# ln(dt) in the bias of the scan's exponential, and plain rows copied by ScalarE

## The chip, the cores and the metric

The kernel runs on one core of one Trainium2 chip. The metric is the device time of one execution in microseconds (us). A core has five engines, each with an instruction queue of its own that is worked off in order: TensorE (PE in the profile; its weight loads are shown apart as PEld), VectorE (DVE), ScalarE (ACT), GpSimd (POOL) and SyncE (SP, which here only issues transfers). They meet at semaphores. SBUF is the working memory, PSUM the memory into which TensorE writes its results.

## The reference

One step of a hybrid encoder layer is computed for 1024 prompt tokens and 64 sample tokens: an input projection, then a state-space scan and a differential attention beside each other, their gated mix, and a feed-forward block with a convolution. The change lies in the scan. Its core in the reference, for one chunk of tokens (`xc` the rows, `dtc` the step sizes, `bc` and `cc` the two state projections):

```python
acum = jnp.cumsum(dtc * a_neg, axis=1)
seg = acum[:, :, None] - acum[:, None, :]
decay = jnp.exp(jnp.where(causal[None, :, :, None, None], seg, -jnp.inf))
xdt = xc * dtc[..., None]
cb = jnp.einsum('blgn,bsgn->blsg', cc, bc)
y = jnp.einsum('blsg,blsge,bsgep->blgep', cb, decay, xdt)
y = y + jnp.einsum('blgn,bgepn->blgep', cc, state) * jnp.exp(acum)[..., None]
to_end = jnp.exp(acum[:, -1:] - acum)
state = state * jnp.exp(acum[:, -1])[..., None, None] + jnp.einsum('blgn,blge,blgep->bgepn', bc, to_end, xdt)
```

The step sizes `dt` are a softplus, so they are positive. There are 32 heads in 4 groups of 8; a head has 64 columns and a state of 64 x 128.

## The kernel before, in words

All data are 32-bit floats. Large products are made of three TensorE products each (high part by high part, high by low, low by high); the scan's own products are plain 32-bit ones.

The program runs through stages. First the input projection, q, k, z and some gates first, in an order of steps written out by hand (`INPUT`): each step sends PE's products and takes out their results on ACT and DVE. Woven into it, by a queue of small jobs (`beside`, `take_turn`), runs `steps` (lines 705 to 754), which makes everything that the scan needs of the step sizes: the softplus into `dt_tok`, the cumulated exponents by a product with a triangle, their negative `nacum` (line 732), the decay of the whole chunk `decs` (line 737), and `dtw`, which is `dt` times the decay to the chunk's end (lines 738 to 740). `dt_tok` and `dtw` are the two halves of one tile `dtt`. The cumulated exponents are also turned and stored to DRAM (`a_sc`, lines 742 to 753). `one_by_one` issues the parts of `steps` one at a time behind a recent copy or read of the projection's results.

Then comes attention, with further tiles of the projection and the convolution woven in (`fill`), and then the scan (lines 1265 to 1447), with gate tiles and two branch products woven in by the same `fill`. The scan goes over 4 groups, and in each over 9 chunks (8 of 128 tokens, one of 64): 36 steps. Each has a front, which runs one step ahead, and a back.

`front` (lines 1287 to 1311): ACT takes the exponential of the row of exponents `bc` that came from `a_sc` (`e2`, line 1294). PE turns the rows of four tiles into one PSUM tile `tr` (line 1297), turns one state projection and multiplies the two into the PSUM tile `cb` (lines 1299 and 1300), which ACT copies (line 1302). DVE multiplies `tr` by `dt` and by `dtw` in one instruction over both halves of `dtt`, which gives `xdt` and `xw`, two halves of the tile `xx` (lines 1303 to 1306; two buffers of it). POOL masks `bc` above the diagonal with -1e30 (line 1307). ACT takes eight exponentials of it, one for each head, with `nacum` as bias (line 1309), and DVE multiplies them by `cb` (line 1310).

`back` (lines 1313 to 1340): PE multiplies `xdt` by the eight decays into `yi` (line 1318) and the old state into `ye` (line 1324); DVE adds the two (lines 1325 and 1326), or ACT copies `yi` where there is no state (line 1328). PE makes the state's addition from `xw` (line 1330); POOL and DVE, or ACT at a group's start, make the new state (lines 1333 to 1337). After three chunks at most `gated`, `normed` and `scaled` finish a span of tokens and store it to `y_sc` (lines 1342 to 1374).

The tiles `tr`, `cb` and `yi` have one PSUM bank each; the woven-in products have three. They share the DVE and ACT queues with the scan: their results are taken out by line 232 (ACT) or 234 (DVE).

The order of the instructions on each engine is drawn up when the kernel is built: the order of the program text gives priorities, `high_priority` raises some, and a simulation with modelled durations decides what each engine issues next. On the chip that order is fixed.

Of the kernel before, what the change touches and what calls it, by code (L numbers as in the profile page):

```python
# [11 lines left out]
AF = mybir.ActivationFunctionType  # L12
ALU = mybir.AluOpType
# [76 lines left out]
def hybrid_layer(ctx: ExitStack, tc: tile.TileContext, xT, xt, prm, cst, rope, wvd, win, wbs, wba, wout, wup, wdn,  # L90
                 ckT, cv, st0, yT, kT, v, ssm, conv, ffn):
    nc = tc.nc
    V, S, G, PE = nc.vector, nc.scalar, nc.gpsimd, nc.tensor
    act = S.activation
# [166 lines left out]
    nacum, decs = (dq.tile([P, 9, 32], F32, name=n) for n in ("nacum", "decs"))  # L261
    dtt = dq.tile([P, 2, 9, 32], F32, name="dtt")
    dt_tok, dtw = dtt[:, 0], dtt[:, 1]
# [12 lines left out]
    def stat(w):  # L276
        t = ps1.tile([P, 512], F32, name="st", tag="st")
        return t[:, :w]
# [197 lines left out]
    def row(tag, name, dt=F32):  # L476
        if tag in ("fa", "fs", "fu"):
            w = {"fa": KT * P, "fs": 4 * P, "fu": HT}[tag]
            return rows_l.tile([P, w], dt, name=name, tag=tag, bufs=IN_ROWS[tag])
        w = {"ss": T}.get(tag, HT)  # L480
        return rows_r.tile([P, w], dt, name=name, tag=tag, bufs=IN_ROWS[tag])
# [223 lines left out]
    def steps():  # L705
        flat = [four[:, 288 * i : 288 * (i + 1)] for i in range(3)] + [row("fx", "dt2")[:, :288]]
        da, e, t, t2 = (x.rearrange("p (a b) -> p a b", b=32) for x in flat)
        u = dtw
        act(e, u, AF.Abs)
        act(e, e, AF.Exp, scale=-1.0)  # L710
        V.tensor_scalar_add(t, e, 2.0)
        V.reciprocal(t, t)
        V.tensor_tensor(out=t, in0=t, in1=e, op=ALU.mult)
        V.tensor_tensor(out=t2, in0=t, in1=t, op=ALU.mult)
        yield
        V.tensor_scalar(e, t2, 1.0 / 17, None, ALU.mult)
        for n in (15, 13, 11, 9, 7, 5, 3):
            V.scalar_tensor_tensor(e, e, 1.0 / n, t2, ALU.add, ALU.mult)
        yield
        V.scalar_tensor_tensor(e, e, 1.0, t, ALU.add, ALU.mult)  # L720
        V.tensor_scalar_max(u, u, 0.0)
        V.scalar_tensor_tensor(dt_tok, e, 2.0, u, ALU.mult, ALU.add)
        an = four[:, 864:896]
        act(an, par[:, O_AL : O_AL + 32], AF.Exp)
        V.scalar_tensor_tensor(da, dt_tok, -1.0, an.unsqueeze(1).to_broadcast([P, 9, 32]), ALU.mult, ALU.mult)
        V.memset(da[TS:, 8, :], 0.0)
        yield
        flat = lambda x: x.rearrange("p a b -> p (a b)")
        pa = stat(288)
        with tc.issue_after(seen["mm"].ins):  # L730
            PE.matmul(pa, tri, flat(da), start=True, stop=True)
        V.tensor_scalar(flat(nacum), pa, -1.0, None, ALU.mult)
        yield
        pl = stat(288)
        with tc.issue_after(seen["mm"].ins):
            PE.matmul(pl, ones, flat(da), start=True, stop=True)
        act(flat(decs), pl, AF.Exp)
        V.tensor_tensor(out=flat(dtw), in0=pl, in1=flat(nacum), op=ALU.add)
        act(dtw, dtw, AF.Exp)
        V.tensor_tensor(out=dtw, in0=dtw, in1=dt_tok, op=ALU.mult)  # L740
        yield
        for c, w in WIDE:
            af = row("fc", "af")[:32, :w]
            pf = stat(512)
            with tc.issue_after(seen["mm"].ins):
                for i in range(c // P, -(-(c + w) // P)):
                    n = min(P, T - i * P)
                    PE.matmul(pf[:32, i * P - c : i * P - c + n], da[:n, i], tri[:n, :n], start=True, stop=True)
            V.tensor_copy(af, pf[:32, :w])
            m = (min(c + w, TP) - c) // P  # L750
            load(out=a_sc[c // P : c // P + m].rearrange("c h t -> h c t"), in_=af[:, : P * m].rearrange("h (c t) -> h c t", t=P))
            if c + w > TP:
                load(out=a_sc[8, :, :TS], in_=af[:, P * m : P * m + TS])
            yield
# [165 lines left out]
    for at, (p, s) in enumerate(rest):  # L920
# [8 lines left out]
        if s == 1 and p in LATER:  # L929
            split_part(LATER[p], seen["copy"], seen["read"])  # L930
    beside = chain(cached_keys(), one_by_one(steps()))
    for n in range(1, len(INPUT)):
        blocks = blocks_of(n + 1) if n + 1 < len(INPUT) else None
# [331 lines left out]
    with (tc.tile_pool(name="sin", bufs=1) as sin, tc.tile_pool(name="sp", bufs=1) as sp,  # L1265
# [21 lines left out]
        def front(g, ch, o, bx, xs, bc):  # L1287
            L = P if ch < 8 else TS
            cs = slice(o, o + L)
            h8 = slice(8 * g, 8 * g + 8)  # L1290
            e2 = sp.tile([P, 4, P], F32, name="e2", tag="e2", bufs=3)
            for u in range(2):
                half = slice(64 * u, 64 * u + 64)
                act(e2[half, :, :L], bc.rearrange("p (j u) t -> p u j t", u=2)[half, u, :, :L], AF.Exp)
            tr = psi.tile([P, 512], F32, name="tr", tag="tr")
            for j in range(4):
                PE.transpose(tr[:L, P * j : P * (j + 1)], xs[:, j, cs], ident)
            cb = psi.tile([P, 512], F32, name="cb", tag="cb")
            PE.transpose(cb[:L, 0:P], bx[:, 0, cs], ident)
            PE.matmul(cb[:L, P : P + L], bx[:, 0, cs], bx[:, 1, cs], start=True, stop=True)  # L1300
            b_cb = sp.tile([P, 2 * P], F32, name="b_cb", tag="b_cb", bufs=3)
            S.copy(b_cb[:L, : P + L], cb[:L, : P + L])
            xx = sp.tile([P, 2, 8, 64], F32, name="xx", tag="xx", bufs=2)
            xdt, xw = xx[:, 0], xx[:, 1]
            tr3 = tr[:L].rearrange("p (e q) -> p e q", e=8).unsqueeze(1).to_broadcast([L, 2, 8, 64])
            V.tensor_tensor(out=xx[:L], in0=tr3, in1=dtt[:L, :, ch, h8].unsqueeze(3).to_broadcast([L, 2, 8, 64]), op=ALU.mult)
            G.affine_select(bc[:L, :, :L], bc[:L, :, :L], [[0, 8], [1, L]], ALU.is_ge, -1e30, base=0, channel_multiplier=-1)
            for e in range(8):
                act(bc[:L, e, :L], bc[:L, e, :L], AF.Exp, bias=nacum[:L, ch, 8 * g + e : 8 * g + e + 1])
            V.tensor_tensor(out=bc[:L, :, :L], in0=bc[:L, :, :L], in1=b_cb[:L, P : P + L].unsqueeze(1).to_broadcast([L, 8, L]), op=ALU.mult)  # L1310
            return L, cs, bc, e2, b_cb, xdt, xw
# [66 lines left out]
        def scan():  # L1378
# [9 lines left out]
            def begin(n):  # L1388
                if n == len(steps):
                    return None  # L1390
                if n and n + 2 < len(steps):
                    asked.append(ask(*steps[n + 2]))
                i, g, c, w, o = steps[n]
                return front(g, (c + o) // P, o, *got[i], asked[n])
# [592 lines left out]
```

## Time and profile before

| | |
|---|---|
| median of 3 runs | 2413.97 us (2413.55 to 2416.66) |
| profiled execution | 2411.51 us, span 2409.7 us |
| instructions | 48636 |
| preparation of the exponents (`steps`) | about 188 to 228 us after the start |
| scan, first to last product of `yi` | 1138.7 to 1467.0 us |

The span goes from the first to the last instruction. The profile's rows give, for a group of instructions, the source line, engine, operation, what is written and read, the count, the busy time and the mean duration of one in ns, and then how long the engine had stood idle just before them and which work ended that idle time. A row of the timeline gives the start and the duration in us. A `q` behind an engine's name is its queue: it waits or issues a transfer, and the engine itself is idle.

### The profile page before, as it was taken

The page shows a single profiled execution, that of the slowest core. Times are in us where ns is not written, and L with a number is a line of the kernel's source. Part 1 is how long each engine was busy: PE and PEld are TensorE (multiplying, and loading weights), DVE is VectorE, ACT ScalarE, POOL GpSimd, SP SyncE. Part 2 cuts the span into 40 slices and gives each one's busy share as a digit, 9 for nine tenths or more (in the row PEclk, how much of TensorE's full clock was granted, in tenths as well). Part 3 has the DMA queues.
Part 4 walks back from the last instruction along what each step waited for, and adds up shares of the span by engine and source line. Part 5 has one row for each costly group of instructions (what it writes and reads, how often), then busy time and mean ns, then how long its engine had stood idle before and what let it go on. Part 6 is the DMA issues. An engine that isn't in the chain of part 4 may idle for free. (4 is left out here: it accounts for less than half of the span.)

```text
span 2409.7 us, 48636 instructions
## 1 busy us (share of the span) xinstructions
PE 2373.4 (98%) x18649; PEld 2302.2 (96%) x18649; DVE 1729.4 (72%) x2938; ACT 1201.2 (50%) x2600; POOL 634.4 (26%) x689
## 2 busy tenths in 40 slices
PE   8999999999999999999999999999999999999998
PEld 8999999999999999999898889999899999999998
DVE  4678887646858768884898886647866667677765
ACT  6444454335656656665566664334443343353442
POOL 0032443320100000001223220012254455443444
PEclk9999999999999999999999999999999999999999
DMA  7873768526554444435978956663124324357876
GB/s 246 273 245 129 266 221 303 170 102 208 160 156 161 151 144 137 148 110 188 353 266 280 331 192 205 203 215 130 65 82 164 138 98 162 127 191 211 246 184 106
DMA packets 288170, 449.74 MB, mean 187 GB/s; under 512 B 35833, under 2 KB 178306, under 8 KB 287938
## 3 DMA queue, kind: packets, MB, share of 16 engines
q1 hardware_dynamic: 258594, 387.00, 48.6%
q0 software_dynamic: 11040, 26.34, 5.4%
q10 hardware_dynamic: 18304, 33.30, 3.7%
q8 instruction: 147, 2.41, 0.4%
q14 instruction: 85, 0.70, 0.1%
HBM read 294.03 MB, written 152.50 MB: 185 GB/s over the span
## 5 line engine op out<-in xcount | busy, mean ns | idle before, releaser
L170 PE MATMUL mm<-b,w_hi 128*128 128x272 f32 x1376 | 407.7, 296 | 0.0
L171 PE MATMUL mm<-b,w_hi 128*128 128x272 f32 x1376 | 405.8, 295 | 0.0
L172 PE MATMUL mm<-b,w_lo 128*128 128x272 f32 x1376 | 403.8, 294 | 0.0
L171 PEld LDWEIGHTS mm<-b,w_hi 128*128 128x128 f32 x1376 | 259.5, 189 | 5.9 <-issue 4.1
L170 PEld LDWEIGHTS mm<-b,w_hi 128*128 128x128 f32 x1376 | 259.3, 188 | 5.3 <-issue 2.7
L172 PEld LDWEIGHTS mm<-b,w_lo 128*128 128x128 f32 x1376 | 259.0, 188 | 5.2 <-issue 4.2
L1629 PE MATMUL mx<-m,w_hi 128*128 128x272 f32 x792 | 152.3, 289 | 2.5 <-DVE hb L1667 1.3
L420 DVE TENSOR_TENSOR wh<-w_f,wh 128x512 fp32r<-128x512 f32 (+1 forms) x156 | 149.7, 960 | 0.7 <-ACT wh L419 0.7
L1629 PE MATMUL mx<-n,wh 128*128 128x272 f32 x1056 | 141.7, 288 | 1.3 <-DVE u L1656 0.9
L1629 PEld LDWEIGHTS mx<-n,wh 128*128 128x128 f32 x1056 | 135.7, 188 | 1.7 <-DVE u L1656 1.2
L1132 ACT ACTIVATE p_t<-sc,mx 128x512 f32<-128x512 f32 (+6 forms) x144 | 106.0, 739 | 59.0 <-DVE mx L1123 33.0
L1629 PEld LDWEIGHTS mx<-m,w_hi 128*128 128x128 f32 x792 | 124.4, 188 | 2.9 <-DVE hb L1667 1.5
L170 PE MATMUL mx<-b,w_hi 128*128 128x272 f32 x416 | 123.4, 297 | 1.1 <-ACT w_hi L155 0.8
L172 PE MATMUL mx<-b,w_lo 128*128 128x272 f32 x416 | 121.6, 294 | 0.0
L563 POOL TENSOR_TENSOR ws<-w_f 128x512 f32<-128x512 f32 (+1 forms) x51 | 69.0, 1354 | 195.4 <-DMA w_f<-in_wdn_dram 84.2
L171 PE MATMUL mx<-b,w_hi 128*128 128x272 f32 x416 | 120.4, 290 | 0.0
L1009 DVE SCALAR_TENSOR_TENSOR cc<-pre,par,cc 128x544 f32<-128x544 f32 (+1 forms) x144 | 111.2, 772 | 8.2 <-ACT cc L1007 6.9
L156 DVE TENSOR_TENSOR w_lo<-w_f,w_hi 128x1024 fp32r<-128x1024 f32 (+1 forms) x74 | 92.5, 1251 | 33.9 <-ACT w_hi L155 33.7
L1629 PE MATMUL mx<-m,w_lo 128*128 128x272 f32 x396 | 114.2, 289 | 0.0
L1638 ACT ACTIVATE cc<-pre,par 128x544 f32<-128x544 f32 (+1 forms) x44 | 37.2, 846 | 150.0 <-DVE pre L1673 149.1
L419 ACT CAST wh<-w_f 128x512 fp32r<-128x512 f32 (+1 forms) x156 | 95.3, 613 | 26.1 <-POOL w_f L569 6.8
L155 ACT CAST w_hi<-w_f 128x1024 fp32r<-128x1024 f32 (+1 forms) x74 | 77.6, 1049 | 56.1 <-PE mm L171 30.3
(466 smaller groups left out, 7124.8 us busy)
## 6 DMA issues: line engine op xcount, KB each, us to landing
w_f<-in_win_dram SPq DMA_DIRECT2D x40, 512.0 KB, 3.9
w_f<-in_wup_dram SPq DMA_DIRECT2D x80, 256.0 KB, 2.6
w_f<-in_win_dram SPq DMA_DIRECT2D x76, 256.0 KB, 3.2
bc<-a_sc SPq DMA_DIRECT2D x32, 512.0 KB, 7.0
b<-y_sc SPq DMA_DIRECT2D x24, 544.0 KB, 8.2
h_sc<-hb SPq DMA_DIRECT2D x44, 272.0 KB, 2.1
ht<-h_sc SPq DMA_DIRECT2D x22, 544.0 KB, 4.6
t_sc<-ht SPq DMA_DIRECT2D x22, 544.0 KB, 3.0
```

What stands on the lines that cost most here:

```text
L155: S.copy(hi, w)
L156: V.tensor_tensor(out=lo, in0=w, in1=hi, op=ALU.subtract)
L170: PE.matmul(ps, a_hi, b_hi, start=i == 0, stop=False)
L171: PE.matmul(ps, a_hi, b_lo, start=False, stop=False)
L172: PE.matmul(ps, a_lo, b_hi, start=False, stop=i == n - 1)
L419: S.copy(hi, src)
L420: V.tensor_tensor(out=lo, in0=src, in1=hi, op=ALU.subtract)
L563: G.tensor_tensor(out=s1, in0=q21, in1=q22, op=ALU.add)
L1009: V.scalar_tensor_tensor(cc[:, :m], pre[:, i : i + m], cw(i), cc[:, :m], ALU.mult, ALU.add)
L1132: act(p_t[:n, :nk], sc[c][:n, :nk], AF.Exp, bias=mx[:n, c : c + 1], accum_out=dst)
L1629: PE.matmul(ps, w[x][:, c], b[y][:, k], start=start and k == i == 0, stop=k == 3 and i == 2, skip_group_check=not start)
L1638: act(cc[:, :n], pre[h][:, :n], AF.Identity, bias=col(O_FB + f), scale=cw(0))
```

## The change

In `steps`, after `dtw` is made, `dt_tok` is raised to at least 1e-37, replaced by its logarithm on ACT, and added to `nacum`. In `front` the exponentials of line 1309 therefore give the decay times `dt`, and `xdt` holds the plain rows: ACT copies them from `tr`. DVE multiplies `tr` only by `dtw`, for `xw`. The shapes of PE's products, the loads and the stores stay as they are.

```diff
         V.tensor_tensor(out=dtw, in0=dtw, in1=dt_tok, op=ALU.mult)
+        V.tensor_scalar_max(dt_tok, dt_tok, 1e-37)
+        act(dt_tok, dt_tok, AF.Ln)
+        V.tensor_tensor(out=nacum, in0=nacum, in1=dt_tok, op=ALU.add)
         yield
...
             xdt, xw = xx[:, 0], xx[:, 1]
-            tr3 = tr[:L].rearrange("p (e q) -> p e q", e=8).unsqueeze(1).to_broadcast([L, 2, 8, 64])
-            V.tensor_tensor(out=xx[:L], in0=tr3, in1=dtt[:L, :, ch, h8].unsqueeze(3).to_broadcast([L, 2, 8, 64]), op=ALU.mult)
+            tr3 = tr[:L].rearrange("p (e q) -> p e q", e=8)
+            S.copy(xdt[:L], tr3)
+            V.tensor_tensor(out=xw[:L], in0=tr3, in1=dtw[:L, ch, h8].unsqueeze(2).to_broadcast([L, 8, 64]), op=ALU.mult)
```

## The prediction

> **What bounds the kernel now.** I read the page's totals first, then the chain that ended last, the stretches around the two places of the change, and the list of who waited for whom.
>
> ```profile
> span 2409.7 us, 48636 instructions
> PE 2373.4 (98%) x18649; PEld 2302.2 (96%) x18649; DVE 1729.4 (72%) x2938; ACT 1201.2 (50%) x2600; POOL 634.4 (26%) x689
> PE 7%; issue 1%; POOL 0%; DVE 0%; POOLq 0%; ACT 0%; DVEq 0%
> ```
>
> PE is busy for 2373.4 of 2409.7 us; 36.3 us is all that it ever stands idle. The chain's shares add up to some 8% of the span: it covers the last 200 us (0.08 x 2409.7), where the scan is long over. So the scan moves the end only by the time that PE loses inside it. The stretches (columns: length, busy time of PE, weight loads, DVE, ACT, POOL, clock, DMA share, GB/s) show how much that is:
>
> ```profile
> 185.00:235.00 50.00, 49.37 (x377) 47.27 (x376) 40.29 (x72) 21.72 (x43) 12.79 (x9) 1.00 0.37 129
> 235.00:640.00 405.00, 402.18 (x3153) 397.59 (x3152) 288.38 (x502) 191.07 (x391) 114.29 (x119) 1.00 0.63 208
> 1121.00:1475.00 354.00, 350.73 (x2849) 314.88 (x2848) 290.37 (x380) 219.27 (x528) 90.78 (x68) 1.00 0.82 277
> ...
> 1201.00:1241.00 40.00, 40.00 (x340) 36.10 (x339) 36.11 (x50) 28.60 (x67) 13.82 (x10) 1.00 0.77 267
> 1241.00:1281.00 40.00, 40.00 (x328) 36.32 (x328) 37.68 (x53) 23.18 (x56) 11.58 (x7) 1.00 0.81 262
> 1281.00:1321.00 40.00, 40.00 (x317) 35.98 (x316) 38.08 (x56) 27.21 (x61) 12.12 (x7) 1.00 0.82 272
> 1321.00:1361.00 40.00, 38.11 (x317) 33.69 (x316) 32.70 (x44) 22.91 (x55) 9.75 (x8) 1.00 1.08 375
> ```
>
> The first row is where the decay's exponents are prepared, the third is the whole scan (36 steps, so 354 / 36 = 9.8 us a step). In the scan PE is idle for 354 - 350.73 = 3.3 us, over half of it in the last row (1.9 us). DVE is the busiest of the others, 290.4 us or 82%, and 90 to 95% between 1201 and 1321; yet PE there shows 40.00 of 40, because the projections that are woven in give it work. ACT has 219.3 us, 62%. The clock is 1.00 throughout. PE's waits in the scan, by who ended them:
>
> ```profile
> PE yi L1318 <- ACT y L1328: 1.9, 1, 1.9
> PE tr L1297 <- DMA in<-x_sc: 0.7, 1, 0.7
> PE yi L1318 <- DVE y L1326: 0.6, 1, 0.6
> ```
>
> These three make 3.2 of the 3.3 us. A lighter DVE can win at most 3.3 us here, 0.14% of 2414. Differences below 0.2% (4.8 us) are about what a measurement of this kernel can't tell from no change.
>
> **The change part by part.** *The preparation.* It adds a maximum and a sum on DVE and a logarithm on ACT, all over 128x288. Their nearest rows:
>
> ```profile
> L711 DVE TENSOR_SCALAR st<-st x1: 301/301/301, 190.6 to 190.6; 128x288 f32<-128x288 f32 x1
> L740 DVE TENSOR_TENSOR dtt<-dtt x1: 674/674/674, 216.8 to 216.8; 128x288 f32<-128x288 f32 x1
> L739 ACT ACTIVATE dtt<-dtt x1: 447/447/447, 216.3 to 216.3; 128x288 f32<-128x288 f32 x1
> 0.74 1.28 ACT L285 ACT_TABLE_LOAD   x1 [0.74 <-PEq L1975]
> 217.87 1.28 ACT L822 ACT_TABLE_LOAD   x1
> ```
>
> DVE gets 0.30 + 0.67 = 0.97 us, ACT 0.45 us. Both table loads name the set of logarithm and exponential, and none lies between them, so the logarithm at about 217.5 finds its table. The stretch 185 to 235 has PE at 49.37 of 50 with DVE at 40.3, ACT at 21.7: both additions lie under it. Behind the new sum on DVE, which waits for the logarithm, stand the copies of line 749, whose PSUM tile the next small product needs. If that cover is gone the cost is the whole detour, 0.97 + 0.45 = 1.4 us, once. The new exponents are first read 900 us later. I take 0; ends 0 and 1.4.
>
> *The rows.* Per step one DVE product of 1024 columns goes; a copy of 512 columns on ACT and a DVE product of 512 columns come. All three read `tr` in PSUM.
>
> ```profile
> L1306 DVE TENSOR_TENSOR xx<-tr,dtt x36: 1206/1216/1226, 1128.8 to 1454.1; 128x1024 f32<-128x1024 f32 x32, 64x1024 f32<-64x1024 f32 x4
> L1325 DVE TENSOR_TENSOR y<-ye,e 128x512 f32<-128x512 f32 x28 | 19.1, 683 | 7.3 <-DMA y_sc<-y 5.2 <-PE ye L1324 2.0
> L1328 ACT COPY y<-yi x4: 578/586/588, 1143.1 to 1394.1; 128x512 f32<-128x512 f32 x4
> L1294 ACT ACTIVATE e<-bc 64x512 f32<-64x512 f32 x64 | 40.2, 629 | 14.1 <-DMA bc<-a_sc 7.4 <-DVE y L1325 5.2 <-DMA o_sc<-ol 1.0
> ```
>
> The remaining product has the form of line 1325, one operand in PSUM and one in SBUF: 0.683 us. DVE saves 36 x (1.216 - 0.683) = 19.2 us and falls to 271.2 us (77%). If the broadcast factor made it as slow as line 1306, the saving would be 0. The copy has the form of line 1328: ACT gets 36 x 0.586 = 21.1 us and rises to 240.4 us (68%). Work on both stays far below 354 us. PE's products, loads and DMAs stay as they are: no queue gets or loses a transfer.
>
> *What the saved DVE time buys.* I looked at the two waits where DVE or ACT held PE up.
>
> ```profile
> 1309.63 1.21 DVE L1306 TENSOR_TENSOR xx<-tr,dtt 128x1024 f32<-128x1024 f32 x1
> 1310.76 0.94 DVE L1371 TENSOR_TENSOR y<-y,zin 128x768 fp32r<-128x768 f32 x1
> ...
> 1310.72 2.31 SPq L214 DMA_DIRECT2D b<-y_sc  x2
> 1313.12 2.75 SPq L1374 DMA_DIRECT2D y_sc<-y  x1
> ...
> 1324.23 0.59 ACT L1328 COPY y<-yi 128x512 f32<-128x512 f32 x1 [4.97 <-DMA y_sc<-y]
> 1324.87 1.09 PE L1318 MATMUL yi<-bc,xx 128*64 128x128 f32 x16 [1.89 <-ACT y L1328]
> ```
>
> The 1.89 us is a chain: the tile `y` had to be stored before ACT could write it anew. DVE was done with it at 1311.70 (1310.76 + 0.94), and would be 0.53 us earlier without the longer product at 1309.63; but the store left SP only at 1313.12, behind two other loads, and landed just ahead of 1324.23, in the stretch whose DMA share is 1.08. DVE isn't what was last, so the gain is 0. The other is 0.60 us at 1429.48:
>
> ```profile
> 1426.18 1.27 ACT L1294 ACTIVATE e<-bc 64x512 f32<-64x512 f32 x2 [2.65 <-DVE y L1325]
> ...
> 1427.52 1.22 DVE L1306 TENSOR_TENSOR xx<-tr,dtt 128x1024 f32<-128x1024 f32 x1
> 1428.66 0.68 DVE L1326 TENSOR_TENSOR y<-y,yi 128x512 f32<-128x512 f32 x1
> ```
>
> Here line 1306 stood ahead of the sum that frees the bank. A product of 0.68 us would end at 1428.20 in place of 1428.74. But if it comes after ACT's copy, which can only start when the pair at 1426.18 ends (1427.45), it starts at 1427.45 + 0.59 = 1428.04 and ends at 1428.72. So 0 to 0.5 us; I take 0. The third wait is for an input's DMA and stays.
>
> *New waits.* The first product `yi` needs ACT's copy and DVE's masked rows; the masked rows come after eight exponentials that stand behind the copy in ACT's queue, so the copy is never the last. `tr` is freed by two engines rather than one: an extra semaphore for PE, at most 36 x 0.051 us = 1.8 us by this row, and the three waits above show none that such an event ended; I take 0.
>
> ```profile
> L1318 PEldq EVENT_SEMAPHORE  x16: 51/51/51, 1162.0 to 1464.3; - x16
> ```
>
> The copy on ACT waits for PE's `tr`; queued behind it are the copy of `b_cb` and the exponentials, and for these wait POOL's next mask and DVE's product. ACT is idle 354 - 240.4 = 114 us in the scan, 3.2 us a step, which hides it.
>
> The sum: 0 + 0 + 0 + 0 on the profiled execution's 2411.51 us (span 2409.7 and 1.8 around it), so 2411.5; the median of the runs shown is 2.5 us higher, 2413.97. I forecast 2414.0 for the median.
>
> **The rivals.** *Slower: the product waits behind the copy.* Both read the same PSUM bank; if the two reads may not overlap, DVE's product starts when ACT's copy ends, and DVE, which works in order, stands still with the filler's evacuations queued behind it. In the Trainium skill, "PSUM — Partial Sum Buffer" (PSUM bank collisions raise a hardware error) says that two engines must not read one bank's quadrant at once; no row of this trace shows it. The place: 1201 to 1321, 12 steps, DVE idle 120 - 111.9 = 8.1 us, after the change 8.1 + 12 x 0.53 = 14.5 us, or 1.2 us a step. At worst the copy stands behind the pair of line 1294: 1.27 + 0.59 = 1.86 us a step, 22.3 us, 7.8 us more than there is. PE would stop for those: 2414.0 + 7.8 = 2421.8 us. It decides from a mean wait of 1.2 us. Against it speak DVE's waits for ACT today on the longer path through the exponentials:
>
> ```profile
> DVE bc L1310 <- ACT bc L1309: 5.9, 5, 2.7
> DVE bc L1310 <- ACT b_cb L1302: 3.8, 2, 3.1
> ```
>
> That is 9.7 us over 36 steps, 0.27 us a step. Chance 0.24.
>
> *Slower: another order of issue.* The order of each engine is drawn up at build time from modelled durations, and three new costs change it in the scan and perhaps behind 217 us. Eight of the nine 40-us pieces lose under 0.8 us each in the present order, one loses 1.9. If half of them lost 1.9, that is 4.5 x 1.9 = 8.5 us against 3.3: 2419 us. For it: only three banks take the filler's results. Against: nothing in the order of PE's own work changes. Chance 0.14.
>
> *Faster.* All 3.3 us go, and PE's sequence closes up besides. "Trainium Kernel Development and Optimization" in the Trainium skill (Performance Expectations) calls matmul busy time a bad metric and the weight loads' share a good one; by it the scan has room, since its loads fill 314.9 of 354 us, 89%, where 235 to 640 reaches 397.6 of 405, 98%. Measured by these rows alone that is 0.982 x 354 - 314.9 = 32.7 us. But much of it isn't waiting:
>
> ```profile
> 1302.71 1.02 PE L1330 MATMUL stp<-xx,b_cb 128*128 128x512 f32 x2
> 1303.15 0.19 PEld L171 LDWEIGHTS mm<-b,w_hi 128*128 128x128 f32 x1 [0.24 <-issue]
> ```
>
> After a pair of state products the loads pause for 0.24 us while PE still streams 512 columns: with 36 pairs 8.6 us that DVE has no part in, and the scan's other small products have shorter pauses of the kind. If a tenth of the 32.7 us could be had, 3.3 us, the time is 2414.0 - 3.3 - 3.3 = 2407.4 us. Chance 0.24.
>
> **How the numbers follow.** No change, 2414.0 us, has the remaining 0.38; its own range is 2410 (all 3.3 us won) to 2418 (1.4 + 1.8 paid). Faster by over 0.2% is the last rival, 0.24; slower the first two, 0.24 + 0.14 = 0.38. The range from 2406 to 2423 holds all four centres with the bounds around them, and leaves about 2 in 10 out at its ends.
>
> **What would show it.** Right: 36 DVE products of 0.68 us and 36 ACT copies of 0.59 us; DVE near 271 and ACT near 240 us in the scan's 354; no table load near 217 us; PE's idle time in the scan near 3 us with the wait at the store of `y` still its largest. Wrong: a wait of the DVE product for ACT's copy of over 1.2 us a step; PE waiting for evacuations; PE's idle time changed by over 5 us, in the scan or in a stage that the change doesn't touch.

## The result, and the profile after

The changed kernel takes 2420.98 us (median of 12 runs, 2414.68 to 2431.81), the kernel before 2413.15 us in the same job (12 runs, 2409.36 to 2417.79). The ratio is 1.0033, with a 95% interval of 1.002 to 1.0046: 7.8 us slower. It lies in the predicted range of 2406 to 2423 us, but the case called likeliest, no change at 2414.0 us, did not come.

The profiled execution took 2426.79 us, with a span of 2424.6 us, 14.9 us more than before. First the totals of its page, then the row of the scan's stretch and PE's waits there (columns as in the prediction):

```profile
span 2424.6 us, 48678 instructions
PE 2382.0 (98%) x18649; PEld 2309.9 (95%) x18649; DVE 1720.3 (71%) x2940; ACT 1219.2 (50%) x2637; POOL 628.1 (26%) x689
```

```profile
1121.00:1475.00 354.00, 345.31 (x2801) 309.58 (x2800) 266.53 (x369) 236.06 (x563) 84.17 (x68) 1.00 0.82 273
```

```profile
PE ye L1328 <- DVE y L1329: 3.2, 2, 2.2
PE cb L1302 <- ACT b_cb L1305: 2.7, 2, 1.5
PE tr L1300 <- DMA in<-x_sc: 2.1, 1, 2.1
PE tr L1300 <- DVE xx L1310: 0.5, 1, 0.5
```

The first two lines split the 14.9 us. PE has the same 18649 products and is busy for 2382.0 us, 8.6 us more; the other 6.3 us is idle time (2424.6 - 2382.0 = 42.6 us against 36.3). The scan's stretch holds 354 - 345.31 = 8.7 us of idle time, where 3.3 us stood before, and no single wait makes it: four different ones do. The largest wait of before, for the store of `y` at 1323, is gone. The largest single wait of the whole neighbourhood lies just past the scan, where PE stands 3.1 us for ACT's cast of a weight part at 1524 (0.8 us before, at 1516):

```profile
PE mx L170 <- ACT w_hi L155: 3.1, 1, 3.1
```

What did the two edited operations cost? These are their groups in the scan; what ended the engine's idle time before them stands last:

```profile
L1310 DVE TENSOR_TENSOR xx<-tr,dtt 128x512 f32<-128x512 f32 (+1 forms) x36 | 24.6, 683 | 12.5 <-ACT xx L1309 12.5
...
L1309 ACT COPY xx<-tr 128x512 f32<-128x512 f32 (+1 forms) x36 | 20.9, 580 | 14.0 <-PE tr L1300 13.7
```

DVE's 36 products fell from 43.8 to 24.6 us, 19.2 us as worked out, and ACT's 36 copies take 20.9 us. DVE's product waits for ACT's copy for 12.5 us, 0.35 us a step.

**Where the idle time comes from.** Up to 1131 us every engine issues its instructions in the same order in both kernels, apart from those of the edit, and behind 1460 us again, but for a handful at about 1710 us. In the scan the orders differ: compared place by place, with the instructions of the edit left out, some 1840 places of PE's sequence hold another instruction, 241 of DVE's, 220 of ACT's and 163 of SP's. One place shows what this does: the tile `y` is written anew after its old content was stored, by the product of `ye` with the exponentials (line 1329, 1325 before). First the store on SP and DVE before, then the same after (start, duration):

```profile
1256.56 0.37 SPq L1374 DMA_DIRECT2D y_sc<-y  x1
...
1256.80 1.22 DVE L156 TENSOR_TENSOR w_lo<-w_f,w_hi 128x1024 fp32r<-128x1024 f32 x1
1257.94 0.55 DVE L257 SCALAR_TENSOR_TENSOR gn<-grs,gn 128x384 f32<-128x384 f32 x1
1258.52 0.56 DVE L258 SCALAR_TENSOR_TENSOR grs<-gn,gn 128x384 f32<-128x384 f32 x1
...
1259.93 2.20 DVE L1362 SCALAR_TENSOR_TENSOR y<-y,par,grs 128x384 f32<-128x384 f32 x4
1262.04 0.69 DVE L1325 TENSOR_TENSOR y<-ye,e 128x512 f32<-128x512 f32 x1
```

```profile
1254.71 0.42 SPq L1378 DMA_DIRECT2D y_sc<-y  x1
...
1256.27 0.42 DVE L234 SCALAR_TENSOR_TENSOR b_g<-b_g,mm 128x272 f32<-128x272 f32 x1
1261.34 0.69 DVE L1329 TENSOR_TENSOR y<-ye,e 128x512 f32<-128x512 f32 x1 [4.65 <-DMA y_sc<-y]
```

Before, DVE had a split of weights, two steps of a norm and the four products by its result ahead of the product that overwrites `y`. The store landed at 1260.38, 3.8 us after its issue, and DVE came to that product at 1262.04 without a wait. After, DVE is free for it at 1256.69, right behind line 234, and the store issued at 1254.71 takes longer, 6.5 us: DVE stands for 4.65 us, and PE, whose next `ye` needs the bank that this product reads, for 2.2 us. Both the earlier place in the order and the slower store have part in this wait; why the store was slower isn't shown. Twenty microseconds on, at the input of the next span, DVE is behind the kernel before: its last reading of the old input ends at 1282.1 (1277.1 before), the load that waits for it is issued at 1282.13, and PE's transposition stands for 2.1 us:

```profile
1282.13 0.80 SPq L1274 DMA_DIRECT2D in<-x_sc  x2
1282.97 0.43 SPq L1275 DMA_DIRECT2D in<-x_sc  x1
...
1289.94 0.63 PE L1300 MATMUL tr<-con,in 128*128 128x128 f32 x4 [2.12 <-DMA in<-x_sc]
```

**Where PE's longer busy time comes from.** Right behind some waits the clock is halved for 3.4 us. These are stretches of the changed kernel that end and begin at the clock's own marks (columns as in the prediction; the clock is the third figure from the end):

```profile
1180.00:1183.20 3.20, 1.39 (x19) 0.88 (x15) 3.20 (x7) 3.18 (x11) 0.24 (x1) 0.99 1.03 354
1183.20:1186.60 3.40, 3.24 (x9) 2.21 (x10) 3.40 (x4) 3.37 (x9) 0.41 (x1) 0.50 1.10 359
1186.60:1190.00 3.40, 3.40 (x29) 3.40 (x28) 3.40 (x5) 2.82 (x7) 0.03 (x1) 1.00 1.09 360
```

PE was idle for 1.81 of 3.20 us, mostly for ACT's copy of `b_cb`; then it worked at half the clock, and a pair of state products took 1.91 us in place of the 1.02 us of the kernel before:

```profile
1182.34 0.30 PE L1302 MATMUL cb<-con,in 128*64 128x128 f32 x1 [1.51 <-ACT b_cb L1305]
...
1184.27 1.91 PE L1334 MATMUL stp<-xx,b_cb 128*128 128x512 f32 x2
```

The trace's clock records show such stretches at 1183, 1528, 1716 and 2193 (the last one twice as long), 17.1 us in sum. In 17.1 us at half the clock PE does some 8.6 us less work: just what its busy time has grown. The profiled execution of before has none before its end, where PE runs dry in every kernel.

Not all of this is the change's doing. The waits at 1716 and 2193 stand in the kernel before too, 12 us earlier. The rows of the first, before and then after:

```profile
1700.00:1710.00 10.00, 8.11 (x60) 7.45 (x60) 10.00 (x18) 4.46 (x7) 0.00 (x0) 1.00 0.26 86
```

```profile
1711.00:1721.00 10.00, 8.16 (x51) 7.72 (x50) 9.96 (x18) 3.93 (x6) 0.27 (x1) 0.83 0.29 102
```

PE idles 1.9 us in one and 1.8 us in the other; the clock is 1.00 in one and 0.83 in the other. So one profile can't say how much the clock takes; the mean granted clock of the timed runs gives an estimate. It is 0.9976 over 28 runs of before and 0.9957 over 7 runs of the changed kernel (below): 0.0019 x 2413 = 4.6 us. Of some 8 us that are lost, more than half would be clock and the rest, some 3.6 us, PE's idle time. It is an estimate of means: single runs don't follow their clock closely. Of the twelve runs of the changed kernel the fastest, 2414.68 us, had 0.994 and the slowest, 2431.81 us, 0.993.

### The profile page after: what moved, and what is told of

Its sections match the earlier page's. It is cut to its first block, busy times and chain, and to the rows that moved or that the text cites. A ratio compares the mean times of both kernels' runs of the same rounds, so it can differ in the third digit from the quotient of the medians.

```text
span 2424.6 us, 48678 instructions
## 1 busy us (share of the span) xinstructions
PE 2382.0 (98%) x18649; PEld 2309.9 (95%) x18649; DVE 1720.3 (71%) x2940; ACT 1219.2 (50%) x2637; POOL 628.1 (26%) x689
## 5 line engine op out<-in xcount | busy, mean ns | idle before, releaser
L156 DVE TENSOR_TENSOR w_lo<-w_f,w_hi 128x1024 fp32r<-128x1024 f32 (+1 forms) x74 | 91.5, 1238 | 35.5 <-ACT w_hi L155 34.9
```

Of the source, the lines that this page charges most:

```text
L156: V.tensor_tensor(out=lo, in0=w, in1=hi, op=ALU.subtract)
```

## The experiments

Two theories at first. The queue theory: the copy on ACT, and DVE's wait for it, hold up the queues. The order theory: the costs of the new instructions make the planner draw up another order for the scan, which meets stores, loads and copies that haven't landed, wherever they happen to lie. Twelve experiments ran. The ratio is to the kernel before as it ran in the same job. "PE idle" is span less PE's busy time, and "half clock" the sum of the halved stretches ahead of the end, both of the profiled execution.

| kernel | median, us | ratio to before, 95% | PE idle | half clock |
|---|---|---|---|---|
| before | 2413.15 | | 36.3 | 0 |
| after | 2420.98 | 1.0033 (1.002 to 1.0046) | 42.6 | 17.1 |
| r1_after_again | 2421.16 | 1.0033 (1.0021 to 1.0045) | 40.1 | 13.7 |
| r2_prep_only | 2413.59 | 1.0001 (0.9989 to 1.0012) | 34.3 | 6.8 |
| r3_dve_copy | 2416.14 | 1.0013 (1.0002 to 1.0025) | 39.0 | 6.8 |
| r4_no_copy | 2420.19 | 1.0035 (1.0023 to 1.0047) | 40.5 | 10.2 |
| r5_before_119 | 2413.13 | 0.9996 (0.9988 to 1.0005) | 34.5 | 3.4 |
| r6_after_119 | 2418.5 | 1.0019 (1.0009 to 1.0029) | 40.7 | 10.2 |
| r7_after_115 | 2426.63 | 1.0054 (1.0039 to 1.0068) | 41.2 | 20.5 |
| r8_swap | 2423.43 | 1.0045 (1.0029 to 1.0061) | 40.4 | 10.2 |
| r9_after_heavy | 2419.79 | 1.0021 (1.0009 to 1.0033) | 37.8 | 10.2 |
| r10_after_y3 | 2423.02 | 1.0035 (1.0021 to 1.0049) | 37.5 | 17.1 |
| r11_after_122 | 2424.24 | 1.0037 (1.0022 to 1.0051) | 46.8 | 17.1 |
| r12_after_gated | 2418.24 | 1.0021 (1.001 to 1.0032) | 35.5 | 20.5 |

In all 14 profiles PE's busy time less half of the half-clock time is between 2369.6 and 2373.5 us. PE's own work is about the same in all; what differs is idle time and clock. Worked out from the mean granted clocks of the timed runs as above, the clock takes more than in the kernel before in all ten kernels with the new instructions in the scan: from 1.2 us (r6) to 6.2 us (r7), and in r12 4.8 of the 5.5 us by which its mean time is longer. In r2 and r5, with the old instructions there, it takes no more than before.

**The changed kernel once more.** No edit.

> The changed kernel again, unaltered. Queue theory (the copy on ScalarE and the product that waits for it hold TensorE up) and order theory (the scan's redrawn order of issue does) agree here: the order is fixed when the kernel is built, so TensorE should again stand idle 8 to 9 us between 1121 and 1475 us (8.7 before in the changed kernel's profile, 3.3 in the kernel before), at the same places, and the time should be about 2421 us. Clock theory (most of the loss is stretches of 3.4 us at half clock, some 1.7 us each): the time goes with the mean granted clock of each run, and a run without such a stretch is within 6 us of the kernel before.

Measured: 2421.16 us, 1.0033. The order of every engine is that of the first build, and the scan's waits come at the same places:

```profile
PE ye L1328 <- DVE y L1329: 2.7, 2, 1.8
PE tr L1300 <- DMA in<-x_sc: 2.1, 1, 2.1
PE cb L1302 <- ACT b_cb L1305: 1.6, 1, 1.6
PE tr L1300 <- DVE xx L1310: 0.5, 1, 0.5
```

So these waits belong to the order, not to the execution. Two others don't return: a second one for the copy of `b_cb`, 1.15 us at 1309 in the first profile, and most of the one for the cast past the scan (0.8 us in place of 3.1). The half-clock stretches differ too: here at 137, 1291, 1714 and 2192, and none at 1183, though PE stands there for the same 2.0 us. That a run's time goes with its clock shows only in part: the run at 0.998 was the fastest of the seven, 2416.35 us, but the one at 0.994 took 2420.87 us, less than the median.

**The preparation alone.**

```diff
--- before
         V.tensor_tensor(out=dtw, in0=dtw, in1=dt_tok, op=ALU.mult)
+        V.tensor_scalar_max(e, dt_tok, 1e-37)
+        act(e, e, AF.Ln)
+        V.tensor_tensor(out=t, in0=nacum, in1=e, op=ALU.add)
```

> The maximum, the logarithm and the sum are made, into tiles that nothing reads, and the scan stays as in the kernel before. Queue theory: no change, 2413 us within 2. Order theory: if these three instructions redraw the scan's order, up to 2421 us with a loss in the scan; if the scan's order stays, 2413 us. If the logarithm needed another table, a table load shows near 217 us and the time stays.

Measured: 2413.59 us, 1.0001 (0.9989 to 1.0012). The scan's order is that of before; two products near 210 us changed places. Neither the three instructions nor the logarithm cost anything that shows, and no table is loaded for it. As nothing waits for them here, they ran earlier than in the changed kernel, the maximum at 209.6 us in place of 219.3; but in the changed kernel too PE is idle for only 0.3 us between 185 and 235 us (0.6 before).

**The copy on DVE.**

```diff
--- after
-            S.copy(xdt[:L], tr3)
+            V.tensor_copy(xdt[:L], tr3)
```

> The changed kernel with the plain copy on VectorE in place of ScalarE: VectorE gets 36 x (0.683 + 0.683 - 1.216) = 5.4 us more than before the change, ScalarE nothing, and no product waits for ScalarE. Queue theory: back to 2413 us within 3, with 3 to 4 us of idle TensorE in the scan. Order theory: the scan is redrawn once more, so the loss can be anything from 2 to 12 us, at places that have nothing to do with the copy: 2412 to 2422 us.

Measured: 2416.14 us, 1.0013 (1.0002 to 1.0025). ACT has its old work and DVE more than before; again the order of the scan is another, and new waits stand in it:

```profile
PE cb L1302 <- ACT grs L1359: 2.3, 1, 2.3
PE mx L170 <- ACT w_hi L155: 1.9, 1, 1.9
PE tr L1300 <- DVE b_g L234: 1.3, 1, 1.3
```

It is the mildest of the changed forms, just clear of no change, but by itself this doesn't tell the theories apart: less ACT work, and another order, both came.

**No copy at all.** `yi` is made from `xw`; the plain rows aren't copied.

```diff
--- after
-            S.copy(xdt[:L], tr3)
...
-                PE.matmul(yi[u : u + 64, e // 2, :L], xdt[:L, e], bc[:L, e, :L], start=True, stop=True)
+                PE.matmul(yi[u : u + 64, e // 2, :L], xw[:L, e], bc[:L, e, :L], start=True, stop=True)
```

> The changed kernel without the copy: the first product reads the rows of the second, so the output is not the reference's. VectorE is 19.2 us lighter than before the change and ScalarE unchanged. Queue theory: the loss is gone, 2410 to 2413 us. Order theory: the relief buys at most the 3.3 us that TensorE was idle in the scan before, and the redrawn order can cost as much as it did in the changed kernel: 2410 to 2422 us, with waits of TensorE for transfers and for tiles that the copy has no part in.

Measured: 2420.19 us, 1.0035 (1.0023 to 1.0047), as slow as the changed kernel without its copy and its wait. The queue theory falls here. The scan's largest waits:

```profile
PE tr L1300 <- DMA in<-x_sc: 5.7, 1, 5.7
PE ye L1327 <- DVE y L1328: 1.7, 2, 1.0
```

The wait from 1283 to 1289 is for the input that PE waited 2.1 us for in the changed kernel. Its load was issued earlier here, from 1279.04, but PE also came to it 4.4 us earlier. 10.2 us at half the clock follow.

**Both kernels with another pace.** `SCAN_STEPS` sets how fast the scan's steps advance against the work woven in; a change of it makes the planner draw up another order. It went from 1.17 to 1.19 in both kernels, and to 1.15 in the changed one.

```diff
-SCAN_STEPS = 1.17
+SCAN_STEPS = 1.19
```

> The kernel before with the rate at which the projections are woven into the scan at 1.19 in place of 1.17: the same work, another order of issue in the scan. Order theory: the loss in the scan moves to other places and by some microseconds, 2410 to 2421 us. Queue theory: the order doesn't matter, 2413 us within 2.

> The changed kernel with the same rate of 1.19: the same instructions in another order. Order theory: a new draw, 2411 to 2424 us, and the waits at 1181, 1260, 1268 and 1288 us of the changed kernel are gone or elsewhere. Queue theory: the load of the copy and its wait are there in any order, so 2419 to 2423 us.

> The changed kernel with the rate at 1.15: one more order of the same instructions. Order theory: 2411 to 2424 us, not the same as at 1.17 and 1.19, and the idle time of TensorE in the scan goes with the time. Queue theory: 2419 to 2423 us.

Measured: the kernel before stays at 2413.13 us (0.9996). Its order is unchanged up to 1321 us; behind that 919 places of PE's sequence hold another instruction, 106 of DVE's and 103 of ACT's, about half of what the change itself moved. The changed kernel takes 2418.5 us at 1.19 and 2426.63 us at 1.15: between two orders of the same instructions lie 8 us, as much as the change itself cost. But the paces reorder less than was expected: at 1.19 and 1.15 the order is that of 1.17 up to 1264 and 1270 us. So the waits near 1181, 1260 and 1268 return in both, and the one near 1288 too (0.7 us at 1.19), where they had been expected to be gone or elsewhere at 1.19. These are the largest at 1.15, for a cast past the scan, the product behind the store, the input and the copy of `b_cb`:

```profile
PE mx L170 <- ACT w_hi L155: 3.3, 1, 3.3
PE ye L1328 <- DVE y L1329: 2.2, 2, 1.2
PE tr L1300 <- DMA in<-x_sc: 1.9, 1, 1.9
PE cb L1302 <- ACT b_cb L1305: 1.5, 1, 1.5
```

**The product ahead of the copy.**

```diff
--- after
-            S.copy(xdt[:L], tr3)
             V.tensor_tensor(out=xw[:L], in0=tr3, in1=dtw[:L, ch, h8].unsqueeze(2).to_broadcast([L, 8, 64]), op=ALU.mult)
+            S.copy(xdt[:L], tr3)
```

> The changed kernel with the two readers of the turned rows in the other order in the program: VectorE's product first, ScalarE's copy after it. Queue theory in its narrow form (the product waits for ScalarE): the product's waits for the copy, 12.5 us in the changed kernel, go, and with them the loss: 2413 to 2416 us. Order theory: the waits change their place, but the scan's order is drawn anew too, so the time is anything from 2411 to 2424 us and doesn't go with these waits.

Measured: 2423.43 us, 1.0045 (1.0029 to 1.0061). DVE no longer waits for the copy; now the copy waits for the product:

```profile
L1309 DVE TENSOR_TENSOR xx<-tr,dtt 128x512 f32<-128x512 f32 (+1 forms) x36 | 24.6, 683 | 8.0 <-PE tr L1300 5.5 <-DMA o_sc<-ol 1.8 <-PE yi L1322 0.6
...
L1310 ACT COPY xx<-tr 128x512 f32<-128x512 f32 (+1 forms) x36 | 20.9, 579 | 16.7 <-DVE xx L1309 16.6
```

With DVE's 12.5 us of waiting for ACT gone the kernel isn't faster: a second count against the queue theory in the form that the product's wait costs the time. (ACT's waits for DVE, 16.6 us, came in exchange.)

By then all six of these changed forms were slower and the three kernels with the old instructions in the scan were not. So I formed a narrower theory: a lighter DVE lets the planner bring the scan's steps forward, to tiles whose store or load isn't done. Four kernels were to show it.

**DVE as heavy as before.** The product is made a second time for six of the eight heads, with the same output.

```diff
--- after
             S.copy(xdt[:L], tr3)
+            V.tensor_tensor(out=xw[:L, :6], in0=tr3[:, :6], in1=dtw[:L, ch, 8 * g : 8 * g + 6].unsqueeze(2).to_broadcast([L, 6, 64]), op=ALU.mult)
```

> The changed kernel with the product made twice for six of the eight heads: VectorE gets 0.55 us a step more (384 columns at 1.04 ns and 0.15 us, worked out from 0.683 us for 512 and 1.216 us for 1024), so its load is that of the kernel before again; ScalarE keeps the copy. Light theory (a lighter VectorE lets the planner bring the scan's instructions ahead, until they stand at tiles whose store or load has not landed): VectorE's wait for the store of y near 1260 us falls from 3 to 4 us to under 1, and the time to 2412 to 2417 us. Queue theory (the copy on ScalarE): 2419 to 2424 us. Order theory without a cause (every redrawn order is a draw): 2411 to 2424 us, with the wait near 1260 us still there or not.

Measured: 2419.79 us, 1.0021 (1.0009 to 1.0033). DVE has its old load in the scan again (295.15 us from 1115 to 1485, where before had 297.82), and the time is still up:

```profile
1115.00:1485.00 370.00, 365.08 (x2928) 326.30 (x2927) 295.15 (x422) 240.92 (x570) 89.43 (x68) 1.00 0.82 271
```

```profile
PE mx L170 <- ACT w_hi L155: 2.7, 1, 2.7
PE yi L1323 <- ACT y L1333: 2.1, 1, 2.1
PE ye L1329 <- DVE state L1342: 1.1, 1, 1.1
```

PE's waits at 1260 and 1288 are gone; others came, at 1160, 1318 and 1519. DVE itself still waits 3.0 us for the store near 1259, where the narrower theory expected under 1 us. So most of the loss doesn't hang on a lighter DVE.

**Three tiles of `y`.** To make room, one buffer less of `grs` and two less of the background's tiles.

```diff
--- after
-BG = 8
+BG = 6
...
-            rs = sp.tile([P, 384], F32, name="grs", tag="grs", bufs=2)[:, :w]
+            rs = sp.tile([P, 384], F32, name="grs", tag="grs", bufs=1)[:, :w]
...
-                    y = sp.tile([P, 4, 384], F32, name="y", tag="y", bufs=2)
+                    y = sp.tile([P, 4, 384], F32, name="y", tag="y", bufs=3)
```

> The changed kernel with three buffers of y in place of two, so that its next span needn't wait for the store of two spans earlier. To make room the tile grs has one buffer in place of two, and the side tiles of the woven-in branches six in place of eight (these can cost some microseconds behind the scan, so TensorE's idle time in the scan is what is read). Light theory: VectorE's waits for the store of y are gone, and with them TensorE's waits for line 1329 near 1260 and 1268 us, about 3 us, and what half clock follows them; the wait for the input near 1290 us stays. Order theory without a cause: other waits of the same sum, 5 to 9 us, take their place.

Measured: 2423.02 us, 1.0035 (1.0021 to 1.0049). No instruction of the scan waits for a store of `y` any more; PE instead stands 4.9 us at 1283 for another copy:

```profile
PE cb L1302 <- ACT grs L1359: 5.1, 2, 4.9
```

The edit takes buffers away too, so it is no clean test of the store alone. It shows that the store's wait isn't needed for the loss.

**A faster pace still.**

```diff
--- after
-SCAN_STEPS = 1.17
+SCAN_STEPS = 1.22
```

> The changed kernel with the weaving rate at 1.22: more projections between two steps of the scan, so the scan runs slower against its transfers. 1.15, 1.17 and 1.19 gave 2426.6, 2421.2 and 2418.5 us. Light theory: the row goes on, 2413 to 2418 us, with less idle time of TensorE in the scan than the 6 to 9 us of the others. Order theory without a cause: no row, 2411 to 2426 us.

Measured: 2424.24 us, 1.0037 (1.0022 to 1.0051). From 1.15 to 1.22 the changed kernel goes 2426.6, 2421.2, 2418.5, 2424.2: no row to follow, where the narrower theory expected 2413 to 2418 us. The scan itself is calmer, but PE stands for 7.5 us at its end, 1490:

```profile
PE gst L1356 <- DVE zin L1352: 7.5, 1, 7.5
PE cb L1302 <- ACT b_cb L1305: 2.8, 2, 1.5
```

**The gating ahead of the rest.**

```diff
--- after
-                    gated(*due)
+                    with tc.high_priority(LAST):
+                        gated(*due)
```

> The changed kernel with the first part of the span's end (gated) raised in priority, so that the input tile it reads last is free earlier and the next input's load leaves SP earlier. Light theory: TensorE's wait for the input near 1290 us (2.1 to 2.3 us) goes, the waits for the store of y stay, 2416 to 2420 us. Order theory without a cause: 2411 to 2424 us, the wait for the input there or not.

Measured: 2418.24 us, 1.0021 (1.001 to 1.0032). PE idles for 35.5 us in the whole execution, less than the 36.3 of before, and is still slower: its clock was halved for 20.5 us. The time lies where both theories had it. PE's wait for the input near 1290 is gone, as the narrower theory said, but so are its waits near 1260, which were to stay. The order is that of the changed kernel up to 1236 us, and the wait of 1.5 us near 1180 returns. This is the longest wait in the scan, and the stretch behind it:

```profile
PE tr L1300 <- DVE xx L1310: 3.9, 2, 3.4
```

```profile
1296.00:1301.80 5.80, 2.42 (x20) 2.23 (x19) 0.96 (x2) 5.58 (x14) 1.09 (x1) 1.00 0.72 237
1301.80:1305.20 3.40, 3.40 (x15) 2.88 (x14) 3.37 (x6) 3.40 (x11) 0.00 (x0) 0.50 0.30 83
1305.20:1310.00 4.80, 4.80 (x45) 4.24 (x43) 4.80 (x8) 3.90 (x7) 3.05 (x1) 1.00 0.40 138
```

**What is settled and what isn't.** Shown: the preparation costs nothing that a measurement shows; neither the copy nor DVE's wait for it is needed for the loss; it goes as PE's waits of 1 to 8 us and as half-clock stretches behind them; two orders of the same instructions differ by 8 us; and where the waits lie depends on the order that the planner drew up (1181, 1260 and 1288 in the changed kernel, 1283 without the copy, 1318 with the heavier DVE, 1490 at pace 1.22). Open: why all ten kernels with the new instructions in the scan were slower, by 3 to 13 us, while the old ones, one of them with a partly new order, were not. The lighter DVE doesn't explain it, since the loss stays with DVE's load restored. A copy on ACT doesn't, since it is there without one. That many orders are possible and the old one is among the good ones would explain it, but one reordering of the old kernel, which moved nothing ahead of 1321 us, is too few to show that; and the changed kernel, its paces 1.15 and 1.19 and the form with the earlier gating have one order up to 1236 us at least, with the wait of 1.5 us for `b_cb` near 1181, so they are not four separate draws. No version beat the kernel before.

## Why the prediction was right or wrong

*PE sets the time, and the scan counts by PE's idle time there.* Half right. The idle time did change by 5.4 us in the scan (3.3 to 8.7; 6.9 us in the second profile), over the 5 us that the prediction named as the mark of its failure. But PE's busy time was taken as fixed, with the clock "1.00 throughout"; it grew by 8.6 us in the profiled execution, and over the timed runs the clock cost an estimated 4.6 us of some 8. The sum has no term for it. That the time still lies in the range is owed to the slower rivals, for whose sake the range reaches to 2423 us; the forecast's own range for no change ended at 2418 us.

*The preparation at 0.* Right: 2413.59 us with it alone, no further table load. Its durations were off, without effect: the maximum took 1.28 us, not 0.30 (0.30 in the kernel with the preparation alone; a POOL operation ran beside it here, from 219.03 to 220.41), and the sum 0.45, not 0.67. The timeline of the changed kernel:

```profile
219.30 1.28 DVE L741 TENSOR_SCALAR dtt<-dtt 128x288 f32<-128x288 f32 x1
...
223.28 0.45 DVE L743 TENSOR_TENSOR nacum<-nacum,dtt 128x288 f32<-128x288 f32 x1
```

*The rows.* Right: 0.683 us a product and 0.580 us a copy. DVE's busy time in the scan is 266.5 us and ACT's 236.1 us, where about 271 and 240 were foreseen.

*The saved DVE time buys 0.* Right in its result: nothing was gained. Its reasoning looked at waits at places that the new order no longer has.

*The semaphore and the new waits at 0.* Right for what it names: PE waits once for DVE's product, 0.5 us. What it left out are waits that come with other places in the queues. It spread ACT's 114 idle us evenly, 3.2 us a step, over the copies; but from 1172 to 1186 ACT's queue has no gap, and there PE waits 1.51 us for the copy of `b_cb`. Whether the new copy, 0.59 us in that queue, has part in this isn't shown; the kernels with the heavier DVE and with three tiles of `y` have the copy on ACT and not this wait.

*The rival of the product behind the copy.* DVE does wait for the copy, 0.35 us a step. It was to decide from 1.2 us, and doesn't. That the time came out near its 2421.8 us is a coincidence, as the kernel without a copy shows.

*The rival of another order.* This is what happened, and here lies the failed step: "Against: nothing in the order of PE's own work changes", with a chance of 0.14 in place of the largest. Nothing in the list of PE's products changes, but their order in the scan does, at some 1840 places. Its price was 8.5 - 3.3 = 5.2 us of idle time; 5.4 us was measured in the first profile and 3.6 us in the second (6.9 us against 3.3, from 1121 to 1475 us). That its 2419 us lies near the measured 2421 us is partly luck: the idle time came out at some 3.6 us of the loss, below the price, and the clock, which the rival doesn't have, added an estimated 4.6 us.

*The rival of a faster kernel.* Wrong: the share of the weight loads in the scan fell from 314.9 to 309.6 of 354 us. PE's idle time, 5.4 us more, explains all of that; a closer sequence didn't come from a lighter DVE.

## What to carry to other kernels

Where a planner draws up the order from modelled costs, an edit of a few instructions is also a new order for everything woven around them, and its price can be that of the waits that the new order meets, not that of the instructions. So test such an edit under several orders (a pace, a priority) before it is judged: here one change measured 2418 to 2427 us. Check, too, from where on these orders differ: two of the paces here left the scan up to 1264 us as it was. And in a kernel that keeps TensorE at 98%, look at the clock behind each wait of over 2 us: it can cost 1.7 us or more on top of the wait itself.

## What the runs showed of the hardware

A wait much shorter than the stretch at half clock can be followed by one. In the 14 profiles there are 94 places ahead of the end where PE idles for over 1.2 us in sum (pauses of over 0.3 us, those less than 3.4 us apart taken together), and 39 of them were followed by a stretch within 4 us. It was 18 of 65 below 2 us in sum, 15 of 23 from 2 to 3 us, and all 6 above 3 us. A stretch lasts 3.4 us or a multiple of that and takes 1.7 us for each 3.4. Whether a given wait is followed by one varies between executions: the same two waits at some 1710 us, 1.8 to 1.9 us in sum, were in 7 of 14. In the Trainium skill, "TensorE: Matmul & The Clock Gate" (What's actually happening) says that the clock falls to half after an idle window of about 3.4 us, and that the window runs freely. The stretches of 3.4 us and the chance in them agree with the free-running window. Read as a window that is idle throughout, the rule doesn't fit, since two waits of 0.99 and 0.61 us at 135 us were enough once, and there the measurement decides.
